# Two-layer trunk in split float32: column blocks of four norms turned through memory, and another order inside the seven-product pairs

## The chip, the cores and the metric

The kernel runs on one core of a Trainium2 chip. The metric is the device time of one execution in microseconds (us); a profiled execution also has a span, from the first to the last instruction of the program. Engines are named as in the profile: PE is TensorE (matrix products), PEld its weight loads, DVE is VectorE, ACT is ScalarE, POOL is GpSimd, SP is SyncE, which issues most transfers (DMAs).

## The reference

Two layers over 256 tokens of width 2048, everything in float32. Layer 0 mixes with a sparse attention and a gated linear attention, layer 1 with a stick-breaking attention. Around the mixers both layers do the same:

```
h = h + mixer(rmsnorm(h))
h = h + (silu(rmsnorm(h) @ w_gate) * (rmsnorm(h) @ w_up)) @ w_down      # FFN_HIDDEN = 5632
h = h + (p[i] @ w_proj) * sigmoid(rmsnorm(h) @ w_pg)
return rmsnorm(h) * final_gain
```

## The kernel before

The stream h (256 tokens as two tiles of 128, by 2048 columns) stays in SBUF with the tokens on the partitions. Every large product is cut into column blocks of 512 and contraction rows of 128. A float32 operand is split into a high part `hi` (rounded to float32r) and the rest `lo`; a product is three matmuls, hi x hi, hi x lo and lo x hi. The weights are split on their way in: SP loads a `raw` tile (4 x 128 rows, 1 MB, `unit`; three such buffers in the feed-forward stages), then for each piece of two rows ACT casts `hi` (`split_sb`, L106) and DVE subtracts `lo` (L107), and PE does 12 matmuls on the piece. There are four buffers each of `hi` (whi) and `lo` (wlo). All engines take their instructions strictly in the order in which they stand; that order comes from a scheduler, which works on its own estimates of when things are ready.

**Norms.** Six norms need their operand with the channels on the partitions: n0 at the start, n1 before the first feed-forward stage (FFN), n2 before the gate of layer 0 (`ple`), n3 before the odd mixer, n4 before the second FFN, n5 before the last gate. When a block `cb` of 512 columns of h is final, `finish_cols` takes its squares on ACT (L116) and queues two calls of `turn_h`. One call does four 128x128 transposes on PE into a PSUM bank (L165), then scales by the gain and splits on ACT (L170) and DVE (L171). Such queued pieces (`later`) are traced one at a time behind a unit of the product that is under way (`tick`), with a delay counted in units; `need` traces them at once.

**Cross.** The hidden layer of the FFN is turned another way (`cross`): DVE transposes 32x32 squares (tq, L143), POOL issues four DMAs to memory (ty, L147) and two back (tx, L151), which permute the squares; then `split_hid` casts on ACT (hH, L921) and subtracts on DVE (hL, L922). tq and tx share one buffer.

**Seven products.** The FFN has 11 column blocks in groups of 3, 3, 3 and 2; from the second group on, the down products of the group before lie between them. Each block b > 0 (`gate_up_7`) does 3 of its 8 row pairs with seven products instead of eight (`pair`, matmuls in L849) and the rest classically. A pair loads gate rows and up rows (two DMAs of 512 KB, L855, gate first), and DVE builds sums of them in `work`: L858 (needs gate and up), L859, L860. Four pieces follow: one raw gate row alone (128x512); sums 1 and 3 (`work`, 128x1024); sums 2 and 4 (`work`); the two up rows (128x1024). Pairs and classical units alternate: P0 C1 P1 C2 P2, then the other classical units, with some adds of partial banks on ACT and DVE (L893 to L902).

Of the kernel before, what the change touches and what calls it, by code (L numbers as in the profile page):

```python
# [19 lines left out]
KC = D // P  # L20
# [7 lines left out]
def trunk_kernel(ctx: ExitStack, tc: tile.TileContext, x, p, even_norm, even_w_in, even_w_gk,  # L28
# [76 lines left out]
    def split_sb(raw, hi, lo):  # L105
        nc.scalar.copy(hi, raw)  # L106
        nc.vector.tensor_tensor(lo, raw, hi.bitcast(F32), OP.subtract)  # L107
# [149 lines left out]

    def finish_cols(nx, cb):

        for tt in range(NT):  # L260
            square_sum(nx["key"], tt, cb, h[:, tt, cb * NB:(cb + 1) * NB])
        for c2 in (2 * cb, 2 * cb + 1):
            later(lambda c2=c2: turn_h(nx["dst"], nx["norm"], c2), key=(nx["key"], c2))
# [443 lines left out]

    def mixer_out(oT, W, nx):
        for i in range(4):
            need(("oT", i))  # L710
        part = {}
        for cb in range(2):
            part[cb] = block(oT, [(W, cb * NB, NB)], k1=8)
        for i in range(4, 8):
            need(("oT", i))
        for cb in range(4):
            ps = block(oT, [(W, cb * NB, NB)], ps=part.get(cb), k0=8 if cb < 2 else 0)
            add_to_h(ps, cb)
            finish_cols(nx, cb)
        for i in range(8):  # L720
            done.pop(("oT", i))
# [105 lines left out]
    def ffn(i, xs, nkey, nx_fn, fp):  # L827
# [23 lines left out]
        def pair(j, b):  # L851

            raw = raw_tile().rearrange("p (r c) n -> p r c n", r=2)
            for c, w in enumerate((ffn_w_gate[i], ffn_w_up[i])):
                nc.sync.dma_start(raw[:, :, c], w[2 * j * P:(2 * j + 2) * P, b * NB:(b + 1) * NB]  # L855
                                  .rearrange("(k q) n -> q k n", q=P))

            nc.vector.tensor_tensor(T[:, 0:2], raw[:, 0], raw[:, :, 1], OP.add)  # L858
            nc.vector.tensor_tensor(T[:, 2], T[:, 1], raw[:, 0, 0], OP.add)  # L859
            nc.vector.tensor_tensor(T[:, 3], T[:, 2], raw[:, 1, 0], OP.add)  # L860

# [3 lines left out]
            def comb(n):  # L865
                return [ST[:, hl, n, j] for hl in range(2)]

            pieces = [(raw[:, 0, 0:1], [(B1, tok(0, 0))]), (T[:, 0:2], [(B5, comb(0)), (B7, comb(2))]),
                      (T[:, 2:4], [(B6, comb(1)), (B4, tok(1, 1))]),
                      (raw[:, 1], [(B2, tok(1, 0)), (B3, comb(3))])]  # L870
            for n, (src, ps) in enumerate(pieces):
                hi = wp.tile([P, 2, NB], F32R, name="whi")
                lo = wp.tile([P, 2, NB], F32R, name="wlo")
                split_sb(src, hi[:, :len(ps)], lo[:, :len(ps)])
                for c, (p, stat) in enumerate(ps):
                    product(p, stat, hi[:, c], lo[:, c], j == 0, j == NS - 1 and p >= B1)
                if n % 2:
                    tick()
# [40 lines left out]
        def split_hid(dst, x, k0):  # L919
            d = [dst[n][:, k0:k0 + 4, :].rearrange("p m (q r) -> p m q r", q=8) for n in range(2)]  # L920
            nc.scalar.copy(d[0], x)  # L921
            nc.vector.tensor_tensor(d[1], x, d[0].bitcast(F32), OP.subtract)  # L922

        def gate_up(gi, n):
# [9 lines left out]
            later(lambda: x.update(x=cross(sl, fp)), key=("xT", i, b))  # L934
            later(lambda: split_hid(hT[gi], x["x"], 4 * n), key=("hT", i, b), after=(("xT", i, b), 16))

        def down(gi, cb, nx):
# [5 lines left out]
            if nx:  # L943
                finish_cols(nx, cb)

# [8 lines left out]
        for cb in range(4):  # L954
            down(len(groups) - 1, cb, nx)
        third["pool"] = None
        return nx

# [20 lines left out]
    def ple(i, xs, nkey, nx, pp, gf=None):  # L979
# [21 lines left out]
        if not last:  # L1001
            for cb in range(4):
                pg = block(xs, [(ple_w_gate[i], cb * NB, NB)], key=nkey)
                rs = rstd_of(nkey)
                for tt in range(NT):
                    gated(pg[tt], tt, cb * NB, NB)
                finish_cols(nx, cb)
            return
# [69 lines left out]
    with tc.tile_pool(name="op", bufs=2) as op:  # L1078
# [3 lines left out]
        nx = start_norm("n4", 4)  # L1082
        mixer_out(oT, odd_w_out[0], nx)
    with tc.tile_pool(name="fp1", bufs=2) as fp:
# [30 lines left out]
```

## Time and profile before

| | |
|---|---|
| Median of 3 runs | 2436.15 us (2432.48 to 2436.17) |
| Profiled execution | 2435.57 us, its span 2433.9 us |
| PE busy | 2393.8 us (98%), 10786 matmuls |
| DVE busy | 1716.8 us (71%) |
| ACT busy | 1258.4 us (52%) |
| POOL busy | 105.6 us (4%) |
| granted TensorE clock, mean | 0.995 |
| DMA | 473 MB, 194 GB/s on average |

Busy time is counted per engine and divided by the span. A time of a stage is read from windows of the span. A matmul's own duration overlaps with its neighbours', so its price is the distance from one start to the next.

### The profile page before, as it was taken

The page shows a single profiled execution, that of the slowest core. Times are in us where ns is not written, and L with a number is a line of the kernel's source. Part 1 is how long each engine was busy: PE and PEld are TensorE (multiplying, and loading weights), DVE is VectorE, ACT ScalarE, POOL GpSimd, SP SyncE. Part 2 cuts the span into 40 slices and gives each one's busy share as a digit, 9 for nine tenths or more (in the row PEclk, how much of TensorE's full clock was granted, in tenths as well). Part 3 has the DMA queues.
Part 4 walks back from the last instruction along what each step waited for, and adds up shares of the span by engine and source line. Part 5 has one row for each costly group of instructions (what it writes and reads, how often), then busy time and mean ns, then how long its engine had stood idle before and what let it go on. Part 6 is the DMA issues. An engine that isn't in the chain of part 4 may idle for free.

```text
span 2433.9 us, 28109 instructions
## 1 busy us (share of the span) xinstructions
PE 2393.8 (98%) x10786; PEld 1965.1 (81%) x10786; DVE 1716.8 (71%) x2009; ACT 1258.4 (52%) x1560; POOL 105.6 (4%) x177
## 2 busy tenths in 40 slices
PE   8999999999999999999999999999999999999998
PEld 7887788778887788888888888887788887888887
DVE  5765556888877877756666666568888788777565
ACT  6644445555545545446546565545554454454463
POOL 0000100100000000000000000000000000000000
PEclk9999999999999999999999999999999999999999
DMA  6454465566666666555554555555666666666563
GB/s 211 146 170 147 147 208 189 194 213 207 213 228 207 208 225 225 196 194 182 176 188 158 169 174 172 193 189 186 203 215 218 217 207 209 223 225 206 183 232 123
DMA packets 240681, 473.13 MB, mean 194 GB/s; under 512 B 12849, under 2 KB 19729, under 8 KB 240418
## 3 DMA queue, kind: packets, MB, share of 16 engines
q1 hardware_dynamic: 232514, 447.07, 55.5%
q0 software_dynamic: 7744, 23.08, 3.0%
q8 instruction: 84, 1.38, 0.2%
q10 hardware_dynamic: 288, 1.18, 0.1%
q14 instruction: 51, 0.42, 0.1%
HBM read 457.66 MB, written 13.63 MB: 194 GB/s over the span
## 4 chain that ended last, share of the span: by engine, by line
PE 71%; DVE 11%; DMA 10%; ACT 3%; issue 3%; SPq 0%; POOL 0%; DVEq 0%; POOLq 0%; ACTq 0%
PE bank L236 20%; PE bank L235 20%; PE bank L237 20%; PE bank L849 6%; DMA raw<-in_ffn_w_up_dram 6%; DVE wlo L107 6%; DMA raw<-in_odd_w_in_dram 2%; ACT whi L106 1%; DVE kT L135 1%; PE bank L165 1%; DVE work L858 1%; DMA raw<-in_ffn_w_down_dram 1%; DMA tx<-ty 1%; DVE sl L931 1%; DVE work L902 1%
## 5 line engine op out<-in xcount | busy, mean ns | idle before, releaser
L107 DVE TENSOR_TENSOR wlo<-raw,whi 128x1024 fp32r<-128x1024 f32 (+2 forms) x848 | 981.7, 1172 | 460.1 <-ACT whi L106 456.4
L106 ACT CAST whi<-raw 128x1024 fp32r<-128x1024 f32 (+2 forms) x848 | 842.3, 1011 | 830.6 <-PE bank L237 542.3
L235 PE MATMUL bank<-whi,aH 128*128 128x512 f32 (+2 forms) x2176 | 849.7, 391 | 0.7 <-ACT whi L106 0.7
L236 PE MATMUL bank<-wlo,aH 128*128 128x512 f32 (+2 forms) x2176 | 843.6, 388 | 5.0 <-DVE wlo L107 5.0
L237 PE MATMUL bank<-whi,aL 128*128 128x512 f32 (+2 forms) x2176 | 842.9, 388 | 0.0
L236 PEld LDWEIGHTS bank<-wlo,aH 128*128 128x128 f32 x2176 | 410.0, 188 | 89.5 <-DVE wlo L107 8.9
L235 PEld LDWEIGHTS bank<-whi,aH 128*128 128x128 f32 x2176 | 409.8, 188 | 84.9 <-issue 2.8
L237 PEld LDWEIGHTS bank<-whi,aL 128*128 128x128 f32 x2176 | 409.4, 188 | 84.9 <-issue 1.0
L235 PE MATMUL bank<-whi,hH 128*128 128x512 f32 x704 | 277.2, 394 | 0.0
L236 PE MATMUL bank<-wlo,hH 128*128 128x512 f32 x704 | 277.0, 393 | 0.0
L237 PE MATMUL bank<-whi,hL 128*128 128x512 f32 x704 | 273.6, 389 | 0.0
L106 ACT CAST whi<-work 128x1024 fp32r<-128x1024 f32 x120 | 126.3, 1053 | 199.5 <-PE bank L237 122.8
L107 DVE TENSOR_TENSOR wlo<-work,whi 128x1024 fp32r<-128x1024 f32 x120 | 146.7, 1222 | 58.0 <-ACT whi L106 57.6
L849 PE MATMUL bank<-whi,sT 128*128 128x512 f32 x480 | 170.2, 394 | 5.5 <-ACT whi L106 5.5
L235 PEld LDWEIGHTS bank<-whi,hH 128*128 128x128 f32 x704 | 132.2, 188 | 30.0
L237 PEld LDWEIGHTS bank<-whi,hL 128*128 128x128 f32 x704 | 132.1, 188 | 29.7
L236 PEld LDWEIGHTS bank<-wlo,hH 128*128 128x128 f32 x704 | 132.4, 188 | 26.1
L849 PEld LDWEIGHTS bank<-whi,sT 128*128 128x128 f32 x480 | 91.2, 190 | 25.3 <-ACT whi L106 6.3
L858 DVE TENSOR_TENSOR work<-raw 128x1024 f32<-128x1024 f32 x60 | 73.4, 1224 | 52.0 <-DMA raw<-in_ffn_w_up_dram 51.6
L147 POOL DMA_DIRECT2D ty<-tq x88 | 48.6, 559 | 1123.3 <-DVE tq L143 973.0
L849 PE MATMUL bank<-wlo,sT 128*128 128x512 f32 x240 | 94.8, 395 | 1.9 <-DVE wlo L107 1.9
L849 PE MATMUL bank<-wlo,aH 128*128 128x512 f32 x180 | 73.3, 407 | 10.8 <-DVE wlo L107 10.4
(253 smaller groups left out, 1623.9 us busy)
## 6 DMA issues: line engine op xcount, KB each, us to landing
raw<-in_ffn_w_down_dram SPq DMA_DIRECT2D x88, 1024.0 KB, 5.4
raw<-in_ffn_w_gate_dram SPq DMA_DIRECT2D x48, 1024.0 KB, 5.2
raw<-in_ffn_w_up_dram SPq DMA_DIRECT2D x48, 1024.0 KB, 5.2
raw<-in_odd_w_in_dram SPq DMA_DIRECT2D x48, 1024.0 KB, 5.1
raw<-in_ffn_w_gate_dram SPq DMA_DIRECT2D x80, 512.0 KB, 4.1
raw<-in_ffn_w_up_dram SPq DMA_DIRECT2D x80, 512.0 KB, 5.3
raw<-in_even_w_in_dram SPq DMA_DIRECT2D x36, 1024.0 KB, 5.1
raw<-in_ple_w_gate_dram SPq DMA_DIRECT2D x28, 1024.0 KB, 5.1
```

Source lines behind the costliest of these rows:

```text
L106: nc.scalar.copy(hi, raw)
L107: nc.vector.tensor_tensor(lo, raw, hi.bitcast(F32), OP.subtract)
L135: nc.vector.transpose(dst[32 * a:32 * a + 32, :, :, 32 * q:32 * q + 32], src.rearrange("p t (m a c) -> p t m a c", a=4, c=32)[32 * q:32 * ...
L147: nc.gpsimd.dma_start(y[:, :, q].rearrange("a c t n -> c a (t n)"), tq[32 * q:32 * q + 32].rearrange("c a t m r -> c a (t m r)"))
L165: nc.tensor.transpose(ps[:, c, tt, :], h[:, tt, k * P:(k + 1) * P], ident)
L235: nc.tensor.matmul(ps[tt][:, :n], sh, hi[:, c, :n], start=st, stop=False)
L236: nc.tensor.matmul(ps[tt][:, :n], sh, lo[:, c, :n], start=False, stop=False)
L237: nc.tensor.matmul(ps[tt][:, :n], sl, hi[:, c, :n], start=False, stop=en)
L849: nc.tensor.matmul(bank[:, p], a, b, start=first and m == 0, stop=last and m == 2)
L858: nc.vector.tensor_tensor(T[:, 0:2], raw[:, 0], raw[:, :, 1], OP.add)
L902: nc.vector.tensor_tensor(e, bank[:, 2 * n:2 * n + 2], e, OP.add)
L931: nc.vector.scalar_tensor_tensor(sl[:, tt], pu[tt], rs[:, tt:tt + 1], sl[:, tt], op0=OP.mult, op1=OP.mult)
```

## The change

It has three parts. First, in n2, n4 and n5 the column blocks 0 and 1, and in n3 the blocks 0, 1 and 2, go through `cross` instead of `turn_h`; `gain_h` then scales and splits from tx, four times 256 columns of ACT (L264) and DVE (L265) for a block. Its ACT instructions, and those of `split_hid`, get an edge without a semaphore that puts them behind the last weight cast traced so far (`state["cast"]`). The down stage and `ple` trace these pieces at the latest at their end (`need`). Second, `split_hid` is traced 10 units behind its cross, not 16. Third, a pair begins with the two gate rows (raw, 128x1024) and ends with the one up row that is left (128x512), and its sums are traced ahead of the pieces that use them; L876, L879 and L880 are the new numbers of L858, L859 and L860.

```
     def split_sb(raw, hi, lo):
-        nc.scalar.copy(hi, raw)
+        state["cast"] = nc.scalar.copy(hi, raw).ins
...
+    def gain_h(dst, norm, x, c2):
+        for k in (2 * c2, 2 * c2 + 1):
+            g = gT[1][:, (norm - 1) * KC + k:(norm - 1) * KC + k + 1]
+            hi, lo = (d[:, k, :].rearrange("p (q r) -> p q r", q=8) for d in dst)
+            with tc.issue_after(state["cast"]):
+                nc.scalar.activation(hi, x[:, k % 4], AF.Copy, scale=g)
+            nc.vector.scalar_tensor_tensor(lo, x[:, k % 4], g, hi.bitcast(F32), op0=OP.mult, op1=OP.subtract)
...
-    def finish_cols(nx, cb):
+    def finish_cols(nx, cb, pool=None):
...
+        if pool:
+            x, first = {}, (nx["key"], "x", cb)
+            later(lambda: x.update(x=cross(h[:, :, cb * NB:(cb + 1) * NB], pool)), key=first)
+            for c2 in (2 * cb, 2 * cb + 1):
+                later(lambda c2=c2: gain_h(nx["dst"], nx["norm"], x["x"], c2), key=(nx["key"], c2),
+                      after=(first, 4))
+            return
...
-            nc.vector.tensor_tensor(T[:, 0:2], raw[:, 0], raw[:, :, 1], OP.add)
-            nc.vector.tensor_tensor(T[:, 2], T[:, 1], raw[:, 0, 0], OP.add)
-            nc.vector.tensor_tensor(T[:, 3], T[:, 2], raw[:, 1, 0], OP.add)
+            def sums_13():
+                nc.vector.tensor_tensor(T[:, 0:2], raw[:, 0], raw[:, :, 1], OP.add)
+
+            def sums_24():
+                nc.vector.tensor_tensor(T[:, 2], T[:, 1], raw[:, 0, 0], OP.add)
+                nc.vector.tensor_tensor(T[:, 3], T[:, 2], raw[:, 1, 0], OP.add)
...
-            pieces = [(raw[:, 0, 0:1], [(B1, tok(0, 0))]), (T[:, 0:2], [(B5, comb(0)), (B7, comb(2))]),
-                      (T[:, 2:4], [(B6, comb(1)), (B4, tok(1, 1))]),
-                      (raw[:, 1], [(B2, tok(1, 0)), (B3, comb(3))])]
-            for n, (src, ps) in enumerate(pieces):
+            pieces = [(None, raw[:, :, 0], [(B1, tok(0, 0)), (B2, tok(1, 0))]),
+                      (sums_13, T[:, 0:2], [(B5, comb(0)), (B7, comb(2))]),
+                      (sums_24, T[:, 2:4], [(B6, comb(1)), (B4, tok(1, 1))]),
+                      (None, raw[:, 1, 1:2], [(B3, comb(3))])]
+            for n, (made, src, ps) in enumerate(pieces):
+                if made:
+                    made()
...
-            nc.scalar.copy(d[0], x)
+            with tc.issue_after(state["cast"]):
+                nc.scalar.copy(d[0], x)
...
-            later(lambda: split_hid(hT[gi], x["x"], 4 * n), key=("hT", i, b), after=(("xT", i, b), 16))
+            later(lambda: split_hid(hT[gi], x["x"], 4 * n), key=("hT", i, b), after=(("xT", i, b), 10))
...
-                finish_cols(nx, cb)
+                finish_cols(nx, cb, fp if cb < 2 else None)
...
+        need((nx["key"], 3))
...
-                finish_cols(nx, cb)
+                finish_cols(nx, cb, pp if cb < 3 else None)
+            need((nx["key"], 5))
...
-        mixer_out(oT, odd_w_out[0], nx)
+        mixer_out(oT, odd_w_out[0], nx, op)
```

**ACT, second seven-product block of the first FFN**, at its third pair P2. `whi<-work` are casts of sums, L893/L916 is the first of the bank adds behind the pair, hH is the cast of the turned hidden block of the block before. Before:

```order
L106 CAST whi<-raw_3769 128x1024 x2
L106 CAST whi<-raw 128x512
L106 CAST whi<-work 128x1024
L921 CAST hH<-tx 128x1024
L106 CAST whi<-work 128x1024
L106 CAST whi<-raw 128x1024
L893 COPY work<-bank 128x512
```

And now:

```order
L106 CAST whi<-raw 128x1024
L106 CAST whi<-work 128x1024 x2
L106 CAST whi<-raw 128x512
L916 COPY work<-bank 128x512
L106 CAST whi<-raw 128x1024
L106 CAST whi<-raw_3873 128x1024
L945 CAST hH<-tx 128x1024
```

The cast from tx stood between the two casts of the sums; now it stands behind all four pieces of the pair and two casts of the next unit.

**DVE, first seven-product block of the first FFN**, at the same pair P2; the row ahead is the last sum piece of P1, `work<-raw` is the first sum of P2. Before:

```order
L107 TENSOR_TENSOR wlo<-work,whi 128x1024 x2
L858 TENSOR_TENSOR work<-raw 128x1024
L107 TENSOR_TENSOR wlo<-raw,whi 128x1024
L107 TENSOR_TENSOR wlo<-raw_3444,whi 128x1024 x2
L859 TENSOR_TENSOR work<-work,raw 128x512
L107 TENSOR_TENSOR wlo<-raw,whi 128x512
```

And now:

```order
L107 TENSOR_TENSOR wlo<-work,whi 128x1024
L876 TENSOR_TENSOR work<-raw 128x1024
L107 TENSOR_TENSOR wlo<-raw,whi 128x512
L879 TENSOR_TENSOR work<-work,raw 128x512
L107 TENSOR_TENSOR wlo<-raw_3444,whi 128x1024 x2
L880 TENSOR_TENSOR work<-work,raw 128x512
```

The first sum of P2 still stands ahead of the last piece of P1, which is now 128x512, and ahead of both pieces of C2.

**ACT, last down stage of the first FFN**, from the squares of block 0 of n2 to those of block 2. Before:

```order
L116 ACTIVATE sqs,ss<-h 128x512 x2
L106 CAST whi<-raw_8087 128x1024 x2
L170 ACTIVATE aH<-bank,gT_94 128x256 x2
L106 CAST whi<-raw 128x1024
```

And now, with the scaling from tx:

```order
L116 ACTIVATE sqs,ss<-h 128x512 x2
L106 CAST whi<-raw_8083 128x1024
L264 ACTIVATE aH<-tx,gT_94 128x256 x4
L106 CAST whi<-raw_8083 128x1024
L106 CAST whi<-raw 128x1024 x2
```

The scaling of a block stood about two casts behind its own squares; now that of block 0 stands one cast behind the squares of block 1.

## Rows read from the trace of the kernel before

**Rows 1.** Windows: length, busy us (count) of PE, PEld, DVE, ACT, POOL; clock, DMA, GB/s

```profile
400.00:1072.00 672.00, 663.30 (x2885) 541.98 (x2884) 519.15 (x528) 332.33 (x352) 40.95 (x66) 0.99 0.64 211
1612.00:2288.00 676.00, 665.13 (x2887) 543.34 (x2886) 520.22 (x528) 333.24 (x353) 40.78 (x66) 0.99 0.64 210
1072.00:1220.00 148.00, 148.00 (x683) 122.27 (x683) 91.39 (x111) 86.22 (x130) 1.42 (x2) 1.00 0.53 178
1546.00:1612.00 66.00, 66.00 (x308) 54.61 (x307) 42.48 (x52) 36.15 (x52) 2.92 (x1) 1.00 0.56 184
2288.00:2340.00 52.00, 52.00 (x244) 42.61 (x243) 31.89 (x44) 33.78 (x58) 0.71 (x1) 1.00 0.50 169
460.00:495.00 35.00, 34.85 (x154) 28.55 (x153) 32.77 (x36) 17.89 (x20) 3.70 (x6) 1.00 0.71 227
```

**Rows 2.** Timeline of PE around one burst of transposes: start, us, instruction

```profile
1077.79 0.39 PE L237 MATMUL bank<-whi,hL 128*128 128x512 f32 x1
...
1078.48 0.39 PE L237 MATMUL bank<-whi,hL 128*128 128x512 f32 x1
1078.71 0.60 PE L165 MATMUL bank<-ident,h 128*128 128x128 f32 x4
...
1079.62 0.39 PE L237 MATMUL bank<-whi,hL 128*128 128x512 f32 x1
```

**Rows 3.** Window, timelines of POOL, ACT, PE, second seven-product block, first FFN

```profile
495.00:512.00 17.00, 14.00 (x49) 10.63 (x48) 11.37 (x13) 7.63 (x9) 0.00 (x0) 0.80 0.56 187
...
493.11 1.50 POOL L151 DMA_DIRECT2D tx<-ty  x2 [6.54 <-DMA ty<-tq]
...
500.57 1.04 ACT L921 CAST hH<-tx 128x1024 fp32r<-128x1024 f32 x1 [5.35 <-DMA tx<-ty]
...
499.88 0.39 PE L849 MATMUL bank<-whi,sT 128*128 128x512 f32 x1
502.61 0.79 PE L849 MATMUL bank<-whi,sT 128*128 128x512 f32 x1 [2.34 <-ACT whi L106]
...
509.64 0.39 PE L237 MATMUL bank<-whi,aL 128*128 128x512 f32 x1
```

**Rows 4.** Timeline of PE, the same place of the second FFN

```profile
1714.36 0.39 PE L849 MATMUL bank<-whi,sT 128*128 128x512 f32 x1
1717.88 0.79 PE L849 MATMUL bank<-whi,sT 128*128 128x512 f32 x1 [3.13 <-ACT whi L106]
...
1724.86 0.40 PE L237 MATMUL bank<-whi,aL 128*128 128x512 f32 x1
```

**Rows 5.** Timelines of DVE and PE, first seven-product block, first FFN, third pair

```profile
447.02 1.23 DVE L858 TENSOR_TENSOR work<-raw 128x1024 f32<-128x1024 f32 x1 [3.59 <-DMA raw<-in_ffn_w_up_dram]
...
449.43 0.50 PE L849 MATMUL bank<-wlo,aH 128*128 128x512 f32 x1 [2.06 <-DVE wlo L107]
```

**Rows 6.** Waits of PE in all: us in total, times, longest us

```profile
PE bank L849 <- DVE wlo L107: 12.3, 17, 3.0
```

**Rows 7.** DVE by form: busy us, mean ns, then idle before

```profile
L107 DVE TENSOR_TENSOR wlo<-raw,whi 128x1024 fp32r<-128x1024 f32 x772 | 931.0, 1221 | 442.5 <-ACT whi L106 439.4
L107 DVE TENSOR_TENSOR wlo<-raw,whi 128x512 fp32r<-128x512 f32 x68 | 46.5, 687 | 9.4 <-ACT whi L106 8.9
```

**Rows 8.** Lines L147, L151, L143: instructions (ns min/median/max); landing of L147's, L151's DMAs

```profile
L147 POOL DMA_DIRECT2D ty<-tq x88: 552/555/755, 438.1 to 2251.6; - x88
DMA to landing us min/median/max: 2.3/2.9/6.1
...
DMA to landing us min/median/max: 3.2/3.5/7.7
...
L143 DVE STREAM_TRANSPOSE tq<-sl x22: 1234/1240/1249, 436.1 to 2248.4; 128x1024 f32<-128x1024 f32 x22
```

**Rows 9.** Timelines of DVE and ACT in the last down stage, first FFN

```profile
1072.88 1.28 DVE L268 TENSOR_TENSOR h<-bank,h 128x512 f32<-128x512 f32 x2
...
1088.06 1.05 ACT L106 CAST whi<-raw 128x1024 fp32r<-128x1024 f32 x1 [0.32 <-PE bank L237]
```

More of the change, by code (lines that the diff above doesn't have):

```diff
@@ L706, in even_mixer, with mixer_out @@
         return oT
-    def mixer_out(oT, W, nx):
+    def mixer_out(oT, W, nx, pool=None):
         for i in range(4):
@@ L718, in mixer_out @@
             add_to_h(ps, cb)
-            finish_cols(nx, cb)
+            finish_cols(nx, cb, pool if cb < 2 else None)
+        if pool:
+            need((nx["key"], 3))
         for i in range(8):
@@ L956, in ffn @@
         third["pool"] = None
+        need((nx["key"], 3))
         return nx
@@ L1006, in ple @@
                     gated(pg[tt], tt, cb * NB, NB)
-                finish_cols(nx, cb)
+                finish_cols(nx, cb, pp if cb < 3 else None)
+            need((nx["key"], 5))
             return
```

## Prediction

> **What bounds the kernel now.** I read the windows of the stages first, then the timelines around the places where PE stands still, then the lines of the turning through memory. In the stages where the four norms are made (last down stages, `ple` of layer 0, the odd mixer's output product) PE is busy for the whole of 148, 66 and 52 us [rows 1]: it is the bound there, so what is taken off PE comes off the time in full, and what ACT, DVE or POOL do beside it is free until PE waits for it. In the two FFNs PE is idle for 672 - 663.3 = 8.7 and 676 - 665.1 = 10.9 us [rows 1], 19.6 together, and the mean clock of 0.99 says that there is something beside the idle time. The reader is to see two kinds of places. In the second seven-product block ACT stands for 5.35 us in front of the cast from tx, which the transfer back (issued at 493.11) delivers only at 500.57, with the cast of the pair's last sums queued behind it; PE then waits 2.34 us, and 3.13 in the second FFN [rows 3, 4]. In the first seven-product block DVE stands for 3.59 us in front of the first sum of P2, whose up rows are there only at 447.02; the `lo` of P1's last piece is queued behind it, and PE waits 2.06 us [rows 5]. The same wait in the second FFN is the longest of the 17 that PE has on this line, 3.0 us [rows 6]. These four waits are 10.5 of the 19.6 us. In the FFN DVE is close behind PE: 32.77 busy of 35 us in one stretch, 519 of 672 on the whole [rows 1].
>
> **The change, part by part.**
>
> *Transposes off PE.* Blocks: 2 each in n2, n4, n5 and 3 in n3, together 9, of 2 bursts of 4 transposes: 18 bursts. Matmuls start every 0.23 us (1077.79 to 1078.48 is three). From 1078.48 to 1079.62 there are three again, and the burst: 1.14 - 0.69 = 0.45 us [rows 2]. 18 x 0.45 = **8.1 us** off a PE that never waits there. I take all of it; the bounds are 8.1 and, if the cost moves to a wait, the rivals below.
>
> *What comes instead.* Nine crosses: DVE 1.24 us each, POOL 4 issues of 0.55 and 2 of 0.75 (1.50 for the two), with landings of 2.9 and 3.5 in the median [rows 3, 8]. DVE is busy for 91 of 148 us and POOL for 1.4 in these stages, ACT for 86 [rows 1], and the gains (L264, L265) do what L170 and L171 did on the same columns; no row of before shows them reading tx, and I give them the same duration. So the cover is PE's own work, and the price is nothing as long as tx is there when ACT comes to it. In the last down stage h of block 0 is final at 1072.88 + 1.28 = 1074.2 [rows 9], and the square transposition stands right behind. In the median tx is there after 1.2 + 2.2 + 2.9 + 1.5 + 3.5 = 11.3 us, with some 0.5 for the handovers 11.8; with the slowest landings of the trace (6.1 and 7.7) after 19.2. By the new order ACT comes to L264 one cast after the squares of block 1, and that cast ran from 1088.06 to 1089.1: 14.9 us after the start. Median transfers come 3 us early, the slowest 4 us late. Then ACT stands, and DVE behind it, but that cast had waited for PE to free a buffer [rows 9], so ACT was ahead by the other three of four buffers, 3 x 12 x 0.23 = 8.3 us of PE's work. Late by 4 costs nothing. In n4 and n5 the order is alike; in n3 the gains stand near the end of the next block's eight casts, later still. The scalings left to PE's turning now fall together behind the last down stage; ACT's surplus there is within the same 8 us. I take **0**, bounds 0 and 5.
>
> *hH behind the casts.* In the second seven-product block of each FFN the cast from tx leaves the place between the two sum casts; what ends its wait (500.57) lies ahead of its new place, which is behind the rest of the pair, the bank add and two casts. ACT's stall of 5.35 us goes, and PE's with all that follows: from 499.88 to 509.64 there are 15 matmul starts, 3.4 us at the pitch, so 9.76 - 3.4 = 6.3 are lost, of which only 2.34 are the first wait. Some of the rest is clock: granted 0.80 on average over these 17 us against 1.00 in the stages of the norms [rows 1, 3], so for a part of them PE ran at 1.2 instead of 2.4 GHz, after it had stood still. At 1714.36 to 1724.86 likewise 10.5 - 3.4 = 7.1 [rows 3, 4]. Together **13.4 us**; what would be late next is P2's `lo`, which DVE makes behind the cast. Lower bound 0 (another wait steps in), upper 13.4. I take 13.4, since the queue behind hH is all that the rows show there.
>
> *Order inside the pair.* The work is the same, the order is not. A pair's last piece is one row now: its `lo` takes 0.69 instead of 1.22 us [rows 7], and PE comes to it three matmuls (0.68) later, since the first piece has twice as many. So where DVE is held up by the sum of the next pair, PE has 0.53 + 0.68 = 1.2 us more before it waits. But at P2 of the first block the first sum still stands ahead of that piece, so the wait for the up rows is not gone: 2.06 and 3.0 us, 5.1 together [rows 5, 6], lose about 1.2 each, and as L859 no longer stands in front of C1, whose buffer the rows are loaded into, the load can go out a little earlier: I take **3.0**, bounds 0 and 5.1. Of the other 19.6 - 10.5 = 9.1 us of idle time in the FFNs, 12.3 - 5.1 = 7.2 are the other 15 waits for `lo` on this line, 0.5 us each on average [rows 6], so most are under the 1.2; I take **6.0**, bounds 0 and 9.1. DVE's small reserve speaks for caution: the sums now stand nearer to the pieces that use them, and hL falls among the bank adds. For waits of that sort I set **2.5** against it, bounds 0 and 6.
>
> *Sum.* 8.1 + 13.4 + 3.0 + 6.0 - 2.5 = 28.0 us. The profiled execution took 2435.57 (span 2433.9), so 2407.6 by it; it stands 0.6 under the median of the runs, so 2408.2 by that. I forecast **2408**.
>
> **The rivals.** A measurement of this kernel can tell about 0.2%, 4.9 us.
>
> *VectorE becomes the bound in the pairs.* With PE no longer stopped by hH, the FFN runs at DVE's rate, and the wait for the up rows returns elsewhere; half of hH's 13.4 comes back and nothing of the rest: 8.1 + 6.7 = 14.8, so 2421. For it: 32.77 of 35 us [rows 1] and DVE idle for 3.6 us in front of the sum. Against it: 519 of 672 over the whole FFN.
>
> *The reorder and hH do nothing that lasts.* Only the transposes count: 2428. For it: the first sum keeps its place ahead of P1's last piece. Against it: hH is demonstrably out of the queue.
>
> *Everything comes back:* 8.1 + 13.4 + 5.1 + 9.1 = 35.7, so 2400. Against it: the sum of P2 still waits for its load.
>
> *Slower: ACT stands in front of the gains.* Place: L264 in the four norms, nine times, with casts and, on DVE, `lo` queued behind it. The price begins when tx comes more than 14.9 + 8.3 = 23 us after the transposition; to eat the other 28 us and 5 more, nine times 3.7 us are needed, so tx at 27. The slowest landings give 19. If each of the six issues on POOL had in addition to wait out two DVE instructions of 1.22 us, 15 us more, it would be 26.5 in the median: nine times 3.5 = 32, so 2440; with slow landings on top, past 2441. What the trace shows of such waits: the 88 issues of ty took 552 to 755 ns, with a median of 555, beside a DVE that is busy for most of the FFN [rows 1, 8]. So nothing was held up, and I give it little.
>
> The Trainium skill, page "SBUF — State Buffer", section "SBUF: two separate sides", warns of just this: a transfer issued from GpSimd has its descriptors written by that engine's cores, which are locked out while DVE runs an instruction that takes both ports, and a transfer of about 620 ns then took about 3100. By that figure, as an estimate, six issues would be 15 us late and the kernel no faster than before; the issues in [rows 8] do not agree with it for the DVE instructions of this kernel.
>
> **How the numbers follow.** Forecast (2401 to 2414 as its own range) 0.57; VectorE's bound 0.20; all back 0.07; transposes alone 0.07; slower 0.05; within 0.2% by a mixture of small losses 0.04. That is faster 0.91, same 0.04, slower 0.05. The range reaches from all back, 2400, to the transposes alone, 2428; it leaves out about 0.13.
>
> **What would show it.** Right: 72 fewer matmuls of L165, and windows of the norm stages with PE busy throughout; no wait of ACT's hH cast on tx in front of work casts, and no clock under 1.00 in the second seven-product blocks; PE's waits in the FFNs down from 19.6 us to 8 or so, the largest left at P2 of the first blocks, behind the sum that waits for the up rows. Wrong: L264 with idle time ended by tx and PE waits behind it; DVE without gaps while PE waits for `lo` all along the pairs; landings of ty and tx longer than 8 us; or PE idle at the start of `ple`, where the scalings crowd.

## The result, and the profile after

The changed kernel takes 2419.68 us in the median of four runs (2419.44 to 2421.38), the kernel before in the same comparison 2436.16 (2432.48 to 2438.87): a ratio of 0.9932, 95% interval 0.9917 to 0.9948. So it is faster by 16.5 us, inside the stated range of 2400 to 2428; the forecast of 2408 had asked for 28. The profiled execution took 2419.45 us with a span of 2417.7. PE has 10714 matmuls in place of 10786, the 72 transposes fewer, and a mean granted clock of 0.998 in place of 0.995.

The windows of the changed kernel, with the columns of [rows 1]; the stages now end 8 to 17 us earlier in the program, so that the end of each window reaches a little into the next stage:

```profile
400.00:1072.00 672.00, 667.75 (x2919) 546.27 (x2918) 527.68 (x533) 341.60 (x359) 43.15 (x70) 1.00 0.65 213
1072.00:1220.00 148.00, 143.72 (x635) 117.75 (x634) 91.69 (x114) 83.00 (x129) 17.80 (x28) 0.99 0.62 211
...
1546.00:1612.00 66.00, 66.00 (x300) 54.65 (x299) 44.82 (x55) 36.81 (x53) 8.18 (x9) 1.00 0.71 236
1612.00:2288.00 676.00, 670.12 (x2925) 547.38 (x2925) 528.58 (x535) 344.18 (x363) 44.48 (x72) 1.00 0.65 213
2288.00:2340.00 52.00, 51.21 (x234) 42.08 (x233) 32.97 (x43) 32.30 (x51) 4.43 (x7) 1.00 0.69 233
...
495.00:512.00 17.00, 16.92 (x75) 13.65 (x74) 16.27 (x18) 11.62 (x13) 0.00 (x0) 1.00 0.61 207
```

In the two FFNs PE is idle for 672 - 667.75 = 4.3 and 676 - 670.12 = 5.9 us, 10.1 together in place of 19.6. The place of the hH stall is full and runs at a granted 1.00 (the last row; 0.80 in [rows 3]). But where the norms are made, PE, which never waited there before, now stands for 4.3 us of the 148 (second row) and 0.8 of the 52.

The waits of PE in the changed kernel (us in total, times, longest), to be read against [rows 6]:

```profile
PE bank L236 <- DVE wlo L107: 9.0, 14, 0.9
PE bank L165 <- DMA h<-in_x_dram: 5.1, 2, 3.0
PE bank L867 <- DVE h L284: 4.6, 7, 1.0
PE bank L165 <- DVE h L1024: 3.1, 1, 3.1
PE bank L235 <- DVE h L284: 1.8, 2, 1.0
...
PE bank L867 <- DVE wlo L107: 0.4, 1, 0.4
```

The last row is what has become of the 12.3 us in 17 waits for `lo` inside the pairs (L867 is the new number of L849). Three rows had hardly any part before: waits for an add to h, 4.6 us at products of a pair (L867), 3.1 at a transpose (L165) and 1.8 in the last down stages (L235). Before, the trace had one of them, 0.5 us.

The lines of the hH cast, of the new gains and of the transfers, in the changed kernel (ns min/median/max; then what the line's engine waited for):

```profile
L945 ACT CAST hH<-tx x22: 1041/1047/1050, 459.4 to 2251.0; 128x1024 fp32r<-128x1024 f32 x22
its engine sat idle before it (us, times) until:
```

```profile
L264 ACT ACTIVATE aH<-tx,gT x36: 492/495/511, 1082.7 to 2307.2; 128x256 fp32r<-128x256 f32 x36
...
its engine sat idle before it (us, times) until:
  DMA tx<-ty: 12.3, 7
```

```profile
L147 POOL DMA_DIRECT2D ty<-tq x124: 552/555/755, 436.9 to 2295.5; - x124
...
DMA to landing us min/median/max: 2.3/3.4/6.5
```

hH waits for nothing any more (the list of the first group is empty). Of the nine crosses' gains seven find tx not there, and ACT stands for 12.3 us in all. The issues of POOL take 555 ns as before, and the landings have a median of 3.4 in place of 2.9 us [rows 8].

**What a late tx costs.** The place is the end of `ple` of layer 0, where the gains of the third block of n3 stand. Timelines of POOL, ACT and PE in the changed kernel (start, us, instruction, what ended its wait):

```profile
1187.41 2.30 POOL L147 DMA_DIRECT2D ty<-tq  x4 [13.11 <-DVE tq L143]
1195.97 1.50 POOL L151 DMA_DIRECT2D tx<-ty  x2 [6.26 <-DMA ty<-tq]
```

```profile
1202.91 1.71 ACT L264 ACTIVATE aH<-tx,gT 128x256 fp32r<-128x256 f32 x4 [3.22 <-DMA tx<-ty]
1204.52 1.04 ACT L106 CAST whi<-raw 128x1024 fp32r<-128x1024 f32 x1
1205.46 1.25 ACT L1021 ACTIVATE sgm<-bank,rstd 128x512 f32<-128x512 f32 x2
```

```profile
1205.17 0.39 PE L237 MATMUL bank<-whi,aL 128*128 128x512 f32 x1
1208.68 1.50 PE L165 MATMUL bank<-ident,h 128*128 128x128 f32 x4 [3.12 <-DVE h L1024]
1209.84 0.78 PE L235 MATMUL bank<-whi,aH 128*128 128x512 f32 x1
1210.41 0.63 PE L236 MATMUL bank<-wlo,aH 128*128 128x512 f32 x1
```

The square transposition began at 1185.88; POOL could issue the two transfers back 6.26 us after its last issue to memory, and the gain began 5.4 us after theirs: 17.0 us in all. ACT stands for 3.22 us in front of the gain. Behind it in ACT's queue are not casts alone but the sigmoids of the last gate block (L1021); the add to h (L1024, on DVE) needs them, and the next transposes of PE (L165) need that h. PE stands for 3.12 us, and then its matmuls start every 0.43 to 0.57 us for a while, so that more than the wait is lost.

### The profile page after: what moved, and what is told of

Same layout as the page of the kernel before. It is cut to its first block, busy times and chain, and to the rows that moved or that the text cites. A ratio compares the mean times of both kernels' runs of the same rounds, so it can differ in the third digit from the quotient of the medians.

```text
span 2417.7 us, 28106 instructions
## 1 busy us (share of the span) xinstructions
PE 2380.8 (98%) x10714; PEld 1953.8 (81%) x10714; DVE 1728.3 (71%) x2018; ACT 1266.1 (52%) x1560; POOL 139.1 (6%) x231
## 4 chain that ended last, share of the span: by engine, by line
PE 72%; DVE 10%; DMA 10%; ACT 3%; issue 3%; POOL 1%; SPq 0%; DVEq 0%; POOLq 0%; ACTq 0%
PE bank L236 20%; PE bank L237 20%; PE bank L235 20%; PE bank L867 8%; DMA raw<-in_ffn_w_up_dram 5%; DVE wlo L107 5%; DMA ty<-tq 1%; ACT whi L106 1%; DMA tx<-ty 1%; DVE work L876 1%; DMA raw<-in_ple_w_gate_dram 1%; DVE tq L143 1%; DVE h L284 1%; DVE work L925 1%; DVE kT L135 0%
## 5 line engine op out<-in xcount | busy, mean ns | idle before, releaser
L236 PE MATMUL bank<-wlo,aH 128*128 128x512 f32 (+2 forms) x2176 | 845.3, 389 | 9.5 <-DVE wlo L107 9.0
L235 PE MATMUL bank<-whi,aH 128*128 128x512 f32 (+2 forms) x2176 | 849.2, 391 | 1.2 <-ACT whi L106 1.2
L236 PEld LDWEIGHTS bank<-wlo,aH 128*128 128x128 f32 x2176 | 409.4, 188 | 100.7 <-DVE wlo L107 20.5
L235 PEld LDWEIGHTS bank<-whi,aH 128*128 128x128 f32 x2176 | 409.3, 188 | 85.5 <-ACT whi L106 2.8
L236 PE MATMUL bank<-wlo,hH 128*128 128x512 f32 x704 | 277.4, 394 | 0.0
L235 PE MATMUL bank<-whi,hH 128*128 128x512 f32 x704 | 276.0, 392 | 0.0
L867 PE MATMUL bank<-whi,sT 128*128 128x512 f32 x480 | 167.5, 389 | 0.0
L147 POOL DMA_DIRECT2D ty<-tq x124 | 68.5, 559 | 1580.7 <-DVE tq L143 1069.2
L235 PEld LDWEIGHTS bank<-whi,hH 128*128 128x128 f32 x704 | 132.1, 188 | 30.9
L236 PEld LDWEIGHTS bank<-wlo,hH 128*128 128x128 f32 x704 | 132.4, 188 | 26.3
L867 PEld LDWEIGHTS bank<-whi,sT 128*128 128x128 f32 x480 | 90.1, 188 | 18.6
L876 DVE TENSOR_TENSOR work<-raw 128x1024 f32<-128x1024 f32 x60 | 73.4, 1223 | 36.5 <-DMA raw<-in_ffn_w_up_dram 36.4
L867 PE MATMUL bank<-wlo,sT 128*128 128x512 f32 x240 | 94.1, 392 | 0.6 <-DVE wlo L107 0.4
L867 PE MATMUL bank<-whi,aH 128*128 128x512 f32 x180 | 70.8, 393 | 4.6 <-DVE h L284 4.6
```

What stands on the lines that cost most here:

```text
L147: nc.gpsimd.dma_start(y[:, :, q].rearrange("a c t n -> c a (t n)"), tq[32 * q:32 * q + 32].rearrange("c a t m r -> c a (t m r)"))
L235: nc.tensor.matmul(ps[tt][:, :n], sh, hi[:, c, :n], start=st, stop=False)
L236: nc.tensor.matmul(ps[tt][:, :n], sh, lo[:, c, :n], start=False, stop=False)
L867: nc.tensor.matmul(bank[:, p], a, b, start=first and m == 0, stop=last and m == 2)
```

## The experiments

All medians and ratios, each ratio against the kernel before on the same chip (its medians there: 2437.72 us for hh_only to late_b2, 2437.33 for after_again to late_both, 2436.92 for idle_cross to n25_late):

| kernel | us | ratio (95%) |
|---|---|---|
| changed | 2419.68 | 0.9932 (0.9917 to 0.9948) |
| hh_only | 2446.66 | 1.0036 (1.0024 to 1.0048) |
| order_only | 2426.81 | 0.9959 (0.9947 to 0.9971) |
| cross_only | 2437.38 | 1.0001 (0.9988 to 1.0013) |
| late_b2 | 2418.21 | 0.9926 (0.9913 to 0.9938) |
| after_again | 2422.18 | 0.9938 (0.9925 to 0.9952) |
| no_cross | 2416.14 | 0.9918 (0.9904 to 0.9931) |
| n3_late | 2420.68 | 0.9933 (0.9921 to 0.9946) |
| late_both | 2414.58 | 0.9910 (0.9896 to 0.9923) |
| idle_cross | 2417.11 | 0.9913 (0.9899 to 0.9927) |
| hh_sums | 2428.44 | 0.9958 (0.9945 to 0.9971) |
| ffn_late | 2414.26 | 0.9905 (0.9891 to 0.9918) |
| n25_late | 2409.85 | 0.9886 (0.9870 to 0.9901) |

Where a difference lies is read from a second table. PE's matmuls stand in one order in a program and, those of L165 left out, there are 10594 of them in each of these kernels; so the time from the start of No. a to the start of No. b in each trace is the time of one stage, whatever happened ahead of it. It comes from one profiled execution of each kernel. In us (n2 is the last down stage of the first FFN with the first proj blocks, n3 the `ple` behind it up to the odd mixer's first units, n4 the odd output product, n5 the second last down stage, end the rest):

| stage (a to b) | before | changed | after_again | no_cross | hh_only | order_only | hh_sums | ffn_late | n25_late |
|---|---|---|---|---|---|---|---|---|---|
| FFN 0 (1800 to 4650) | 664.4 | 656.7 | 655.6 | 655.1 | 671.8 | 659.8 | 659.9 | 654.4 | 653.9 |
| FFN 1 (6960 to 9900) | 689.3 | 680.4 | 684.8 | 679.7 | 695.2 | 683.5 | 683.5 | 676.8 | 676.0 |
| n2 (4650 to 4920) | 65.4 | 64.8 | 63.6 | 65.4 | 65.4 | 65.4 | 65.4 | 65.4 | 64.4 |
| n3 (4920 to 5370) | 105.4 | 108.0 | 107.5 | 105.4 | 105.4 | 105.4 | 105.4 | 105.4 | 105.4 |
| n4 (6720 to 6960) | 57.3 | 55.4 | 59.0 | 57.3 | 57.3 | 57.3 | 57.3 | 57.3 | 57.3 |
| n5 (9900 to 10140) | 58.7 | 57.7 | 56.7 | 58.7 | 58.7 | 58.7 | 58.7 | 58.7 | 56.7 |
| end (10140 to 10593) | 82.3 | 83.8 | 83.6 | 82.3 | 82.3 | 82.3 | 84.1 | 82.3 | 82.3 |

What the expectations call the ledger is this count, made first for the kernel before and the changed one. The first 50 us hold no edit, and still matmul No. 203 starts at 48.7 us in one of these traces and at 52.0 in another; so two totals that differ by 3 us say little, while the rows of n2 to n5 without an edit agree to 0.1. The end does not always: hh_sums takes 84.1 there without an edit of it.

**The parts one by one.** Three kernels take the kernel before and one part of the change each. hh_only, whose edit is

```
-        nc.scalar.copy(hi, raw)
+        state["cast"] = nc.scalar.copy(hi, raw).ins
...
-            nc.scalar.copy(d[0], x)
+            with tc.issue_after(state["cast"]):
+                nc.scalar.copy(d[0], x)
...
-            later(lambda: split_hid(hT[gi], x["x"], 4 * n), key=("hT", i, b), after=(("xT", i, b), 16))
+            later(lambda: split_hid(hT[gi], x["x"], 4 * n), key=("hT", i, b), after=(("xT", i, b), 10))
```

> The kernel before with only the edge and the 10 units of the cast hH. Theory of the ledger (the three parts add up, and this one is worth what PE lost at 499.88 and 1714.36): 13.4 us less than before, 2422.8, with ACT's waits of 5.35 and 6.13 us on tx gone and the clock at 1.00 there. Rival (the parts need each other: without the other order inside the pair the wait goes over to the lo of the pair's last piece, which still has 128x1024): less than 8 us, over 2428, with a PE wait on DVE of more than 2 us in the second seven-product blocks.

It is slower than before by 0.36%. Timeline of DVE in its second seven-product block, and PE behind it:

```profile
493.59 0.69 DVE L860 TENSOR_TENSOR work<-work,raw 128x512 f32<-128x512 f32 x1
497.24 1.23 DVE L858 TENSOR_TENSOR work<-raw 128x1024 f32<-128x1024 f32 x1 [2.97 <-DMA raw<-in_ffn_w_up_dram]
498.39 1.22 DVE L107 TENSOR_TENSOR wlo<-work,whi 128x1024 fp32r<-128x1024 f32 x1
499.52 3.49 DVE L107 TENSOR_TENSOR wlo<-raw,whi 128x1024 fp32r<-128x1024 f32 x3
```

```profile
496.77 0.40 PE L849 MATMUL bank<-whi,sT 128*128 128x512 f32 x1
499.66 0.79 PE L849 MATMUL bank<-wlo,sT 128*128 128x512 f32 x1 [2.49 <-DVE wlo L107]
500.25 0.63 PE L849 MATMUL bank<-whi,sT 128*128 128x512 f32 x1
...
505.73 0.40 PE L237 MATMUL bank<-whi,aL 128*128 128x512 f32 x1
```

The cast from tx has left its place, but in the new order the first sum of the next pair (L858) stands right behind L860, ahead of four `lo`; in the kernel before it stood behind them, at 492.83, and waited for nothing. Now it waits 2.97 us for up rows, PE waits 2.49 us for the `lo` behind it, and its matmuls start every 0.43 us until 505.7. Counted as what the starts lie further apart than the pitch of 0.227 us, this loses 5.4 to 6.6 us in the second and in the third such block of each FFN, 12 in an FFN, where the stall of hH had lost 6.4 and 7.1. The rival had the place right, though not that the part alone would be a loss.

order_only takes from the change's diff the lines of `pieces`, `sums_13` and `sums_24`, and leaves hH as before:

> The kernel before with only the other order inside the pairs. Theory of the ledger (the waits for lo behind late up rows get shorter by some 1.5 us in each first block, most of the small ones go, but the product into B2 now stands second in a block and waits for the add of the down product that reads the same bank, 7 times 0.5 to 1.1 us): 2 to 4 us less than before, 2432 to 2434, with the 7 waits of PE on the add to h in the trace. As the prediction had it: 6.5 us less, 2429.6, and no such waits. Rival (VectorE bounds the pairs whatever their order): within 1 us of before.

It is faster by 10.9 us, more than either theory said. Its longest waits of PE in the FFNs:

```profile
PE bank L849 <- DVE h L268: 6.5, 8, 1.3
...
PE bank L849 <- ACT whi L106: 3.3, 2, 2.6
PE bank L849 <- DVE wlo L107: 3.2, 4, 1.0
```

The waits for `lo` fall from 12.3 to 3.2 us, those for the add to h come up as the theory of the ledger said, and hH still stops PE twice (3.3). By the stages 10.4 us are gained: 1353.64 - 1343.26 in the two FFNs.

cross_only takes those of `finish_cols`, `gain_h` and `need`, so the crosses of n2 to n5 and nothing else:

> The kernel before with only the column blocks of n2 to n5 turned through memory. Theory of the ledger (PE saves 8.2 us at its bursts, but loses 5 at the end of ple of layer 0 where ACT stands in front of a gain for tx with the sigmoids of the last block queued behind it, and some 3 more where ple begins, in front of late loads): within 1.5 us of before, 2435 to 2437. As the prediction had it (the gains are covered): 8.1 us less, 2428. Rival (late gains alone, the loads at the start of ple have nothing to do with it): 3 us less, 2433.

No change that can be measured, as the theory of the ledger had it. Together the three parts alone give +8.9 - 10.9 - 0.3 = -2.3 us, the change -16.5: they don't add up, since hH's part turns from a loss into a gain where the order inside the pairs is there.

**What the sums' place does.** hh_sums is hh_only with the two functions `sums_13` and `sums_24` called ahead of their pieces, and the old pieces:

```
...
             for n, (src, ps) in enumerate(pieces):
+                if n in (1, 2):
+                    (sums_13, sums_24)[n - 1]()
...
```

> The kernel before with the edge of hH and with sums traced ahead of the pieces that use them, but the old order of the pieces (one gate row first, the two up rows last) and no crosses. Theory (the edge alone lost because the sum of the next pair came to stand four instructions earlier on DVE, in front of the lo of the pair under way, and waited there for up rows; the place of the sums mends that): 15 us or more less than before, under 2422, and no wait of PE on DVE of more than 1.5 us in the second and third seven-product blocks. Rival (it takes the new order of the pieces too, with the short piece last): within 5 us of the edge alone, over 2438.

2428.4, between the two theories: 18 us less than the edge alone. In the FFNs it takes 1343.4 us; hh_only took 1367.0, and with the new pieces as well (no_cross) it is 1334.8. So of the 32 us between the edge alone and the edge with the whole new order the place of the sums gives 24 and the new pieces 9 in these traces. The 24 is on the high side, as hh_only's profiled execution was the slowest of its nine, 5 us over their median; by the ratios it is 19 and 10 of 29. The theory's second sign did come: no wait of PE on DVE in the second and third blocks is over 0.5 us. What stays is the wait at P2 of the first blocks (PE waits for its `lo` for 3.3 us at the longest) and many small ones:

```profile
PE bank L849 <- DVE wlo L107: 9.9, 9, 3.3
PE bank L236 <- DVE wlo L107: 7.2, 17, 1.3
```

**The wait for the add to h.** In the changed kernel the second product of a block goes to the bank B2, which is the one that the last down product left its sums in. Timelines of DVE and PE at the start of such a block:

```profile
635.00 1.23 DVE L876 TENSOR_TENSOR work<-raw 128x1024 f32<-128x1024 f32 x1 [1.62 <-DMA raw<-in_ffn_w_up_dram]
636.15 1.22 DVE L107 TENSOR_TENSOR wlo<-work,whi 128x1024 fp32r<-128x1024 f32 x1
637.28 1.28 DVE L284 TENSOR_TENSOR h<-bank,h 128x512 f32<-128x512 f32 x2
```

```profile
636.79 0.39 PE L867 MATMUL bank<-whi,aL 128*128 128x512 f32 x1
638.02 0.50 PE L867 MATMUL bank<-whi,aH 128*128 128x512 f32 x1 [0.85 <-DVE h L284]
```

late_b2 moves that product behind those into B5 and B7, in the first pair of a block:

```
-                for c, (p, stat) in enumerate(ps):
-                    product(p, stat, hi[:, c], lo[:, c], j == 0, j == NS - 1 and p >= B1)
+                todo = [(p, stat, hi[:, c], lo[:, c]) for c, (p, stat) in enumerate(ps)]
+                if j == 0 and n == 0:
+                    held = todo.pop()
+                if j == 0 and n == 1:
+                    todo.append(held)
+                for p, stat, hc, lc in todo:
+                    product(p, stat, hc, lc, j == 0, j == NS - 1 and p >= B1)
```

> The changed kernel, in which the first pair of a block does its product into B2 behind those into B5 and B7 instead of second; nothing else moves. Theory (the 7 waits of PE on the add to h come from the bank alone: the add is there 1.4 us later at the latest): 4 to 5 us less than the changed kernel, 2415 to 2416, and no wait of PE on the add to h at a product of a pair. Rival (VectorE is behind anyway, and PE then waits as long for the lo of the next piece): within 1 us of the changed kernel, 2419 to 2420.5.

The seven waits are gone from its trace, and its FFNs take 1332.7 us in place of 1337.1, but the time, 2418.2, does not stand clear of the changed kernel's. The same edit without crosses (ffn_late, below) shows what it gives: 3.6 us less in the FFNs than no_cross (1331.2 against 1334.8).

**What the crosses cost.** after_again is the changed kernel, and no_cross has the three calls of `finish_cols` as before, of which one stands here, and no `need` behind them; both ran on one chip:

```
-                finish_cols(nx, cb, fp if cb < 2 else None)
+                finish_cols(nx, cb)
```

> The changed kernel itself once more, as the measure for the three kernels beside it on the same chip. Both theories: as in its first comparison with the kernel before, a ratio of 0.992 to 0.995.

> The changed kernel without its first part: all blocks of n2 to n5 are turned by PE again, the edge of hH and the order inside the pairs stay. Theory (what PE saves by the crosses, 8.2 us, it loses again in the gate stages, as the part alone came to no change): within 2 us of the changed kernel. As the prediction had it (the crosses are worth 8.1 us): 8 us over the changed kernel.

Without crosses the kernel takes 2416.14 us (four runs, 2415.83 to 2417.54), with them 2422.18 (five runs, 2419.36 to 2424.43): the crosses make it slower by 6.0 us, or by 3.5 against the first measurement of the changed kernel, which neither expectation had. idle_cross keeps the nine square transpositions and all their transfers, lets PE turn the blocks all the same, and lets nobody read tx:

```
-            for c2 in (2 * cb, 2 * cb + 1):
-                later(lambda c2=c2: gain_h(nx["dst"], nx["norm"], x["x"], c2), key=(nx["key"], c2),
-                      after=(first, 4))
-            return
```

> The changed kernel in which PE turns all blocks again as in the kernel without crosses, and the nine crosses of n2 to n5 run all the same, square transposition and transfers, but their results are read by nobody (gains L264 and L265 are left out). It tells what the crosses cost apart from the wait of the gains. Theory of the gains (what the crosses lose, they lose where ACT stands for tx with adds and sigmoids behind it): as without crosses, 2416 to 2418. Rival (their transfers make weight loads late, and POOL and DVE work does the rest): 4 us or more over it, 2420 to 2424.

2417.1, as without crosses, with 124 issues of POOL in the trace. So the transfers and the work of DVE and POOL cost no time by themselves, and the loss comes only with the gains that read tx. The transfers do make weight loads late. Waits of ACT's casts on the gate weights of `ple` in no_cross, idle_cross and the changed kernel (us in total, times, longest):

```profile
ACT whi L106 <- DMA raw<-in_ple_w_gate_dram: 24.2, 14, 3.9
ACT whi L106 <- DMA raw<-in_ple_w_gate_dram: 38.0, 16, 3.5
ACT whi L106 <- DMA raw<-in_ple_w_gate_dram: 42.5, 16, 4.7
```

PE does not feel this in idle_cross, where n3 takes 105.4 us as in no_cross. But the casts have less lead over PE: in n3 they wait for PE to free their buffers for 31.2 us in no_cross, 18.3 in idle_cross and 9.4 in the changed kernel. Whether that takes part in the loss was not tried apart. n3_late moves one group of gains, the worst:

```
...
-                finish_cols(nx, cb, pp if cb < 3 else None)
-            need((nx["key"], 5))
+                finish_cols(nx, cb, cp if cb < 3 else None, 10 if cb == 2 else 4)
...
```

> The changed kernel, in which the gains of block 2 of n3 are traced 10 instead of 4 units behind their cross, so that on ACT they stand behind the sigmoids of the last gate block (the cross of n3 gets a pool of its own that outlives the stage). Theory (ACT stands 3.2 us for tx in front of those sigmoids, and PE then waits 3.1 us and more for h at the first transposes behind the stage): 4 to 5 us less than the changed kernel, and no wait of PE on the add to h there. Rival (the weight loads of the stage are late because the crosses take from the same transfers, so that PE waits for casts instead): within 1.5 us of the changed kernel, with PE waits on ACT's casts in their place.

In the trace n3 takes 104.6 us, 2.8 less than in after_again and 0.8 less than with PE's own transposes, and the wait of L165 there is gone. The waits on casts that the rival asked for did not come in its place, though the loads are as late as before; two on the scalings of the last block did, 1.0 and 0.6 us. By the whole time, 2420.68, it is not clear of after_again, because n4 and the second FFN vary by as much from run to run (n4: 55.4 in one profiled execution of the changed kernel, 59.0 in the other, where ACT stood for 4.26 us in front of the gains of n4's second block). late_both has both mends:

> The changed kernel with both mends, the later product into B2 and the later gains of n3. Theory (two places that have nothing to do with each other): the sum of what each gives by the traces, 4 to 6 and 4 to 5, so 8 to 11 us less than the changed kernel, 2409 to 2412 where that stands at 2419.7. Rival (VectorE and the loads are close behind PE, and each wait that goes lets another come up): not more than 5 us less.

2414.58, 7.6 us less than after_again: a little under the 8 to 11 that the theory gave, and over the 5 of the rival.

**A faster kernel.** ffn_late has the edits of no_cross and of late_b2; n25_late keeps the crosses of n2 and n5, and against the changed kernel differs, beside the late B2, by

```
-                finish_cols(nx, cb, pp if cb < 3 else None)
-            need((nx["key"], 5))
+                finish_cols(nx, cb)
...
-        mixer_out(oT, odd_w_out[0], nx, op)
+        mixer_out(oT, odd_w_out[0], nx)
```

> The changed kernel without the crosses of n2 to n5, with the later product into B2. Theory (both count in full): 4 to 6 us less than without crosses alone, 2410 to 2412, the least of all so far. Rival (the wait for the bank goes over to the lo behind it): 2415 to 2417.

> The changed kernel with crosses in n2 and n5 alone (the two that lie in the last down stages), none in n3 and n4, and with the later product into B2. Theory (only where PE alone bounds the stage and nothing stands behind the gains is a cross worth its 0.9 us a block; by the stages of the profiles n2 and n5 gain 1 to 2 us each, and lose 1 at the end of the kernel): 1 to 3 us less than the kernel without any cross and the same B2, so 2407 to 2411. Rival (a cross is worth nothing anywhere): the same as that kernel or up to 2 us more.

ffn_late takes 2414.26 us (2413.38 to 2415.70), 1.9 less than no_cross by the medians, 3.2 by the ratios, so a little under what the theory said. n25_late takes 2409.85 (2408.74 to 2411.35) and is the fastest of all, 4.4 us under ffn_late on the same chip and 9.8 under the changed kernel. n2 and n5 give 1.0 and 1.9 us of that by the stages, the FFNs 1.3; the loss of 1 at the end of the kernel that the theory set against it did not come (82.3 us). Its windows, and its gains:

```profile
400.00:1072.00 672.00, 670.01 (x2931) 548.81 (x2930) 528.22 (x535) 340.78 (x360) 43.08 (x70) 1.00 0.65 214
1612.00:2288.00 676.00, 673.83 (x2945) 551.24 (x2944) 533.53 (x543) 345.94 (x372) 46.59 (x76) 1.00 0.65 214
```

```profile
L264 ACT ACTIVATE aH<-tx,gT x16: 492/495/511, 1077.9 to 2298.3; 128x256 fp32r<-128x256 f32 x16
...
its engine sat idle before it (us, times) until:
  DMA tx<-ty: 2.5, 3
```

PE is idle for 4.2 us in the two FFNs, and ACT stands for tx 2.5 us in all.

## Why the prediction held its range and missed its value

- *The place and the pairs, 13.4 + 3.0 + 6.0 - 2.5 = 19.9 us.* Right as a sum: with both and no crosses the kernel is faster by 21.2 us (2437.33 to 2416.14), by the stages of the FFNs 18.8. The stall of hH is gone in the size forecast: the 15 starts that took 9.76 and 10.49 us take 3.4 in the changed kernel, 6.4 and 7.1 us less. The place of P2 in the first blocks gave 4.0 us where 3.0 were forecast. In the pairs the waits for `lo` fell by 11.9 us (12.3 to 0.4); against them stand 4.0 more at L236, in front of the classical units (5.0 to 9.0), and 4.1 for adds to h at products of a pair (0.5 to 4.6). The first is of the sort for which 2.5 was set; the second was not seen, though the bank of B2 can be read in the code.
- *That the two are separate terms* was wrong. "Lower bound 0 (another wait steps in)" was too mild: the wait that steps in, the sum in front of up rows, is the one that the prediction knew from the first block, and alone with it the part loses 8.9 us. The order pays twice, for itself and as what lets hH's part count: alone it gives 10.4 to 10.9 us where 6.5 were forecast, and hH on top of it 8.5 to 10.7 where 13.4 were. The two misses offset each other, so that the sum fits is in part luck.
- *Transposes, 8.1 us.* Right in size: 72 fewer, and at each burst's place the way from the matmul ahead of it to the third behind it is 0.45 us shorter. Where no wait follows, a stage has the saving in full: n4 of the changed kernel 1.9 us, n5 of after_again 2.0, with 1.8 forecast for each.
- *Crosses at 0, bounds 0 and 5.* This is the step that failed, and it makes up the miss: with 8.1 us saved and a loss of 3.5 to 6.0 on balance they cost 12 to 14 us, where the value is off by 11.7. By the stages of the two traces of the changed kernel, n2 to n5 together give 1.0 and 0.1 us in place of 8.1 (n3 alone loses 2.5 and 2.0), so 7 to 8 us of the cost lie there; 1.5 and 1.3 lie at the end of the kernel, where cross_only and n25_late lose nothing and the cause is open; most of the rest is in the FFNs (last point). Two things were wrong in the step. The estimate of 11.8 us added medians of single transfers; a cross waits for the last of four and then for the last of two, 6.26 and 5.4 us in the place shown in place of 2.9 and 3.5. From L143 to the first gain the nine took 13.5 to 17.0 us. ACT was there after 13.1 to 15.1 (forecast 14.9), and in n3 after 13.8 to 14.0, not "later still"; so in seven of nine it stood, for 0.6 to 3.2 us. That much the prediction had allowed: its slowest transfers came 4 us late. What failed above all is "Late by 4 costs nothing". It counted as cover the buffers of the weight casts, 8.3 us; the sigmoids behind the gains on ACT, and the adds to h behind L265 on DVE, have no buffers, and PE asks for their h at its next transposes. That is the slower rival's mechanism at a smaller size: ACT stood for 12.3 us over nine blocks, where the prediction asked for 33 (nine times 3.7) to make the kernel clearly slower.
- *The rival nearest in number*, VectorE as the bound (2421), did not come by its mechanism: it left the FFNs half of hH's 13.4, 6.7 us, and nothing of the order, and they gained 16.5 us in the changed kernel and 18.8 in no_cross. That 2419.7 lies beside 2421 is chance.
- *Of the rival's second half*, in which each issue on POOL waits out instructions of DVE, nothing came: 124 issues took 552 to 755 ns, median 555, as in [rows 8]. The Trainium skill, page "SBUF — State Buffer", section "SBUF: two separate sides", has a transfer issued from GpSimd that takes about 620 ns alone take about 3100 while DVE runs a `tensor_copy`. DVE's instructions beside the crosses are sums and differences of two operands, scalings and square transpositions; beside these the trace shows no such delay of the issues, and the page's own case was not run here.
- *What would show it.* The 72 fewer matmuls, the hH cast without a wait and the clock of 1.00 came; norm stages with PE busy throughout did not. PE's idle time in the FFNs was to fall to 8 or so and fell to 10.1; the largest of it was to be the sum at P2, and is the many waits for `lo` of classical units and for the add to h. Of the signs for wrong, the first came: "L264 with idle time ended by tx and PE waits behind it".
- *Open:* in its two profiled executions the changed kernel takes 2.3 and 5.6 us more in the FFNs than no_cross (1337.1 and 1340.4 against 1334.8). In the first FFN, which ends ahead of the first cross and has one order of PE, DVE and ACT in both kernels, it is 1.6 and 0.5 us, so that much comes without the crosses. In the second FFN, behind whose first rows the order is the same too, it is 0.7 and 5.1; of the 5.1, 3.3 lie around one wait for an add to h, 2.2 us long with slow matmuls behind it, at a place where no_cross waits 0.3. With the later product into B2 that wait is gone, and the FFNs take 1332.7 (late_b2) and 1331.9 us (late_both) with crosses, 1331.2 (ffn_late) without. Whether the crosses make the wait longer, or it varies by itself, single traces don't tell.

## What to carry to other kernels

Before a piece of work is moved off the bound engine, list everything that stands behind its waiting instruction in that queue, and separate what has buffers in front of the bound engine (weight casts) from what it asks for directly (sums to h, sigmoids): only the first is cover. A chain of several transfers is costed by the last landing of each set, not by the median of one. Terms that lie in one in-order queue are tried together as well as alone: here the same edit was a loss of 9 us or a gain of 8.5 to 10.7 by what stood beside it.

## What the runs showed of the hardware

The same program does not start alike: matmul No. 203, which no edit touches, starts at 48.7 to 52.0 us in the traces, and 20 runs of the kernel before on one chip went from 2428.8 to 2442.8 us.

A stop of PE can cost more than its length, by slow matmuls behind it. In hh_only PE waits 2.49 us, and its matmuls then start 0.43 us apart, in place of 0.23, until 6 us later. The windows of hh_only around the stop and of its slow part alone, with the columns of [rows 1]:

```profile
495.00:512.00 17.00, 14.07 (x48) 10.55 (x47) 10.61 (x11) 7.66 (x10) 1.50 (x2) 0.80 0.48 155
500.20:505.40 5.20, 5.20 (x14) 3.99 (x13) 5.04 (x7) 1.66 (x2) 0.00 (x0) 0.50 0.74 214
```

The granted clock of the slow part is 0.50, so 1.2 in place of 2.4 GHz, and the stop costs 5.6 us in all. Not every stop does this: the wait of 2.06 us in [rows 5] costs 2.3 us, and the clock from 446 to 458 us of that trace is 1.00. What tells the two kinds apart is not shown.
